# The gate tiles of the value pass: one split for each pair, ordered in the first of its two blocks

## The chip, the cores and the metric

The kernel runs on one core of a Trainium2 chip. The metric is the time of one execution in device microseconds (us), where lower is better. The engines are named as the profile names them: PE (TensorE, with PEld for its weight loads), DVE (VectorE), ACT (ScalarE), POOL (GpSimd) and SP (SyncE, which here only issues DMAs). Each engine works through its own instructions in the order in which the program issued them; an instruction whose inputs or buffer aren't ready holds up everything behind it on that engine.

## The reference, cut to what matters

Two trunk layers run over 256 prompt tokens and 32 sample tokens (8 sequences of 4). Each layer ends in a PEER mixer, which is where the change lies:

```python
q = (xb @ w_q).reshape(PEER_BLOCK, N_PEER_HEADS, 2, HALF_KEY)
s = jnp.einsum('thpd,hpnd->thpn', q, keys)
v1, i1 = lax.top_k(s[:, :, 0], TOPK_HALF)
v2, i2 = lax.top_k(s[:, :, 1], TOPK_HALF)
...                                         # 16 best of the 256 pairs: expert (128*i1 + i2), gate g
u = u_tab[expert]
v = v_tab[expert]
act = jax.nn.gelu(jnp.einsum('td,thkd->thk', xb, u), approximate=False)
return jnp.einsum('thk,thkd->td', g * act, v)
```

There are 16384 experts, 8 heads and 16 experts for each head and token. A table of experts has rows of 1024 numbers.

## The kernel before, in words

For 248 of the prompt tokens (`ND`, the "dense columns") the kernel does not gather experts. It computes the activation of every expert for every token as a dense product, multiplies by a gate that is zero where the expert wasn't chosen, and multiplies by the whole value table. The other 8 prompt tokens and the 32 sample tokens are done with gathered rows ("extra" and "sample").

**Blocks.** The tables come as 128 blocks of 128 experts, 512 KB each. Each block is split into two fp32r halves: ACT writes the high half `wh` (L234, cast) and DVE the low half `wl` (L235, subtract). The matmuls then run three times, high by high, high by low and low by high. There are three buffers for `wh` and `wl`; when block i is taken, block i+2 is split, so the ACT cast for i+2 waits until PE is done with block i-1.

**The U pass** (`kind == "u"`) multiplies block j of the first table by the 248 tokens: 24 matmuls of 128x248 into `pu` (L463 to L465). After each second block ACT applies the Gelu and writes the two columns of experts into `store` (L1340).

**The gates.** `gphase(c)` for the three chunks of blocks 0 to 45, 46 to 91 and 92 to 127 builds one-hot matrices of the chosen experts on DVE (`build`: L1249, L1251, L1253), multiplies them on PE into `pgt` (L1273, L1275) and multiplies `store` by the result on DVE (L1282). One round of matmuls for two groups of tokens and the DVE work on it is called a burst.

**The V pass** (`kind == "v"`) needs `store` as the moving operand, again in two halves: `wsplit(j)` writes `gh` (ACT, L439) and `gl` (DVE, L440) for blocks j and j+1 at once, 128x496, into one of two buffers each, and enters both halves of the pair in the list `gw`. `vmm` then does the 24 matmuls of a block (L1317 high, L1318 with `gl`, L1319 with `wl`) into four accumulators `acc`.

**The order of the blocks**, from `peer_order`: 82 U blocks (`RING`, the size of `store`), then two V and two U blocks in turn until U is at its end, then V alone. Blocks 126 and 127 of V are multiplied in the end stage (`vlast`).

**What sets the order of the rest.** After every block `pump` is called. It keeps two clocks of its own, `tp` for what PE has been given (2690 ns for a block) and `td` for what DVE has been given (1200 for a block, 620 for a `wsplit`, and a cost for each background step). While `td` is behind `tp` it issues the next background step: of the gate phases (`self.bg`), and, when those have to wait or are done, of the extra and sample work (`self.bg2`); in some blocks one step of the latter is issued in any case. So a DVE instruction stands in DVE's queue where `pump` or the block loop put it.

In the loop before, `wsplit(j - j % 2)` is called at the start of each V block. It does nothing when `j` is in `gw`. After a block `gw.pop(j)` takes the entry away, so at the start of an odd block the entry of the even one is missing and the pair is split a second time; then `wsplit(j + 1)` splits the next pair.

Of the kernel before, what the change touches and what calls it, by code (L numbers as in the profile page):

```python
# [201 lines left out]
class Stream:  # L202
# [39 lines left out]
    def next(self, src, idx, look=2):  # L242
        i = self.use_n
        self.use_n += 1
        assert self.items[i][0] is src and self.items[i][1] == idx, (i, self.items[i][1], idx)
        while self.split_n <= min(i + look, len(self.items) - 1):
            self._split()
        return self.hl.pop(i)


def peer_order():
    order = [("u", j) for j in range(RING)]
    u, v = RING, 0
    while v < 128:
        order += [("v", v), ("v", v + 1)]
        v += 2
        if u < 128:
            order += [("u", u), ("u", u + 1)]
            u += 2
    return order  # L260


class Kern:
# [867 lines left out]
    def peer(self, l):  # L1131
# [159 lines left out]
        gw = {}  # L1291

        def wsplit(j):
            c = [i for i, (j0, j1) in enumerate(CHUNKS) if j0 <= j < j1]
            if j in gw or not c or G[c[0]] in self.bg:
                return
            wh = wp.tile([128, 2, ND], F32R, name="gh", tag="gh", bufs=2)
            wl = wp.tile([128, 2, ND], F32R, name="gl", tag="gl", bufs=2)
            self.split_act(wh, wl, store[:, j % RING:j % RING + 2])
            self.td += 620  # L1300
            for i in range(2):
                gw[j + i] = (wh[:, i], wl[:, i])
# [8 lines left out]
        def vmm(j, w, d):  # L1311
            wh, wl = gw[j]
            vh, vl = w
            o = acc[d // 2][:, d % 2, :ND]
            f = j == 0 and d % 2 == 0
            e = j == 127 and d % 2 == 1
            nc.tensor.matmul(o, vh[:, d], wh, start=f, stop=False, skip_group_check=True)  # L1317
            nc.tensor.matmul(o, vh[:, d], wl, start=False, stop=False, skip_group_check=True)  # L1318
            nc.tensor.matmul(o, vl[:, d], wh, start=False, stop=e, skip_group_check=True)  # L1319

        for kind, j in peer_order():
            if kind == "v":
                if l == 0 and j in ADJ:
                    next(self.fg)
                for c, (j0, j1) in enumerate(CHUNKS):
                    if j == j0:
                        self.flush(G[c])
                wsplit(j - j % 2)
                if j % 2:
                    wsplit(j + 1)  # L1330
            if j >= 126 and kind == "v":
                continue
            w = self.wnext()
            if kind == "u":
                if j % 2 == 0:
                    pu = ps.tile([128, 2, NP], F32, name="pu", tag="mm", bufs=2)
                self.mm3(pu[:, j % 2, :ND], w, [(k, k) for k in range(KT)], aH, aL, 0, ND, True, True)
                if j % 2:
                    s = j % RING - 1
                    nc.scalar.activation(store[:, s:s + 2], pu[:, :, :ND], AF.Gelu)  # L1340
                done["u"] = self.udone = j + j % 2
                self.td += 1200
            else:
                if acc is None:
                    self.von = True
                    acc = [ps.tile([128, 2, NP], F32, name=f"acc{i}", tag="acc", bufs=4) for i in range(4)]
                for d in range(KT):
                    vmm(j, w, d)
                gw.pop(j)
                self.td += 1200  # L1350
            self.tp += 2690
            self.pump()
# [207 lines left out]
```

## Time and profile before

| | |
|---|---|
| median of 3 runs | 2377.87 us (2373.52 to 2379.7) |
| the profiled execution | 2358.28 us, of which the trace spans 2356.5 us |
| mean granted PE clock, profiled execution | 0.964 |
| first layer: U pass alone, then V pass | about 260 to 515 us, then 515 to 1164 us |
| second layer: U pass alone, then V pass | about 1432 to 1680 us, then 1680 to 2324 us |

The times are those of one core, and the profile is of one execution. In a row that groups instructions, the first number after the bar is their busy time in us, the second the mean of one in ns, and after the next bar stands how long their engine had been idle just before them and what ended that. In a row of a stretch of time, the numbers behind the length are the busy us of each engine (with the count), the granted PE clock as a share of full speed, the share of time in which the DMA engines were busy, and GB/s.

### The profile page before, as it was taken

How to read it: one execution, taken by the hardware profiler on the slowest of the kernel's cores; microseconds unless marked ns; L12 is line 12 of the kernel's file. 1: busy time of each engine (PE TensorE's matmuls, PEld its weight loads, DVE VectorE, ACT ScalarE, POOL GpSimd, SP SyncE). 2: the span in 40 equal slices, each digit the busy share in tenths (PEclk: the TensorE clock that was granted, in tenths of full speed). 3: DMA queues.
4: the chain of work that ended last, by engine and by line, in shares of the span. 5: the costliest groups of instructions: out<-in, count | busy, mean ns of one | idle time of the engine just before them, and what ended most of it. 6: DMA issues, size and time to landing. Idle time of an engine off the chain costs nothing. (4 is left out here: it accounts for less than half of the span.)

```text
span 2356.5 us, 46884 instructions
## 1 busy us (share of the span) xinstructions
PE 2085.2 (88%) x19266; PEld 1940.0 (82%) x19266; DVE 1752.2 (74%) x3496; ACT 981.7 (42%) x1341; POOL 256.9 (11%) x313
## 2 busy tenths in 40 slices
PE   7998999998888967788988889999988988778887
PEld 3787999998888857788976679999988888777887
DVE  3777997887777756678675679988876778666785
ACT  1845444344433323344441544444443434333443
POOL 1100004001000010012012100040020100000220
PEclk9999999999999989999999999999998999899998
DMA  9773458557665665569569645585575666544682
GB/s 356 267 285 131 148 193 287 171 171 232 208 203 192 204 197 153 161 196 325 152 185 280 225 131 155 186 302 171 170 255 177 213 200 211 158 129 125 226 287 82
DMA packets 131815, 477.11 MB, mean 202 GB/s; under 512 B 16032, under 2 KB 16544, under 8 KB 130960
## 3 DMA queue, kind: packets, MB, share of 16 engines
q1 hardware_dynamic: 93168, 334.09, 44.5%
q0 software_dynamic: 38432, 140.03, 17.8%
q8 instruction: 151, 2.47, 0.4%
q14 instruction: 64, 0.52, 0.1%
HBM read 466.63 MB, written 7.39 MB: 201 GB/s over the span
## 5 line engine op out<-in xcount | busy, mean ns | idle before, releaser
L235 DVE TENSOR_TENSOR wl<-raw,wh 128x1024 fp32r<-128x1024 f32 x583 | 708.3, 1220 | 324.3 <-ACT wh L234 323.4
L234 ACT CAST wh<-raw 128x1024 fp32r<-128x1024 f32 x583 | 609.7, 1047 | 637.9 <-PE acc L1318 411.3
L1318 PE MATMUL acc<-gl,wh 128*128 128x248 f32 x2048 | 603.7, 295 | 179.6 <-DVE gl L440 179.6
L1317 PE MATMUL acc<-gh,wh 128*128 128x248 f32 x2048 | 590.6, 288 | 7.7 <-ACT gh L439 7.7
L1319 PE MATMUL acc<-gh,wl 128*128 128x248 f32 x2048 | 589.0, 288 | 0.0
L465 PE MATMUL pu<-aH,wl 128*128 128x248 f32 x2048 | 569.7, 278 | 9.0 <-DVE wl L235 8.9
L1318 PEld LDWEIGHTS acc<-gl,wh 128*128 128x128 f32 x2048 | 406.6, 199 | 204.4 <-DVE gl L440 204.4
L463 PE MATMUL pu<-aH,wh 128*128 128x248 f32 x2048 | 573.3, 280 | 0.0
L464 PE MATMUL pu<-aL,wh 128*128 128x248 f32 x2048 | 571.1, 279 | 0.0
L1317 PEld LDWEIGHTS acc<-gh,wh 128*128 128x128 f32 x2048 | 406.7, 199 | 10.8 <-ACT gh L439 9.1
L1319 PEld LDWEIGHTS acc<-gh,wl 128*128 128x128 f32 x2048 | 407.5, 199 | 0.0
L465 PEld LDWEIGHTS pu<-aH,wl 128*128 128x128 f32 x2048 | 388.7, 190 | 10.8 <-DVE wl L235 10.7
L463 PEld LDWEIGHTS pu<-aH,wh 128*128 128x128 f32 x2048 | 387.3, 189 | 2.5 <-issue 2.1
L464 PEld LDWEIGHTS pu<-aL,wh 128*128 128x128 f32 x2048 | 388.0, 189 | 0.0
L439 ACT CAST gh<-store 128x496 fp32r<-128x496 f32 x254 | 153.2, 605 | 159.6 <-PE acc L1319 159.6
L440 DVE TENSOR_TENSOR gl<-store,gh 128x496 fp32r<-128x496 f32 x254 | 162.6, 668 | 21.1 <-ACT gh L439 20.7
L1340 ACT ACTIVATE store<-pu 128x496 f32<-128x496 f32 x128 | 74.9, 585 | 238.7 <-PE pu L465 238.7
L1282 DVE SCALAR_TENSOR_TENSOR store<-pgt,store 128x100 f32<-128x100 f32 (+3 forms) x192 | 86.8, 496 | 53.3 <-PE pgt L1275 52.4
L463 PE MATMUL prj<-aH,wh 128*128 128x288 f32 x392 | 119.9, 306 | 2.3 <-ACT wh L234 2.3
L1251 DVE TENSOR_TENSOR oA<-c,iT 128x1280 f16<-128x1280 f16 (+2 forms) x142 | 120.5, 849 | 0.0
L1369 POOL DMA_INDIRECT grow<-ur,ei x64 | 62.6, 978 | 514.4 <-DVE grow L1452 419.6
L464 PE MATMUL prj<-aL,wh 128*128 128x288 f32 x392 | 116.9, 298 | 0.0
(366 smaller groups left out, 2634.5 us busy)
## 6 DMA issues: line engine op xcount, KB each, us to landing
raw<-ut SPq DMA_DIRECT2D x256, 512.0 KB, 4.0
raw<-vt SPq DMA_DIRECT2D x256, 512.0 KB, 4.1
adaw<-wada POOLq DMA_DIRECT2D x56, 512.0 KB, 7.5
raw<-w SPq DMA_DIRECT2D x54, 512.0 KB, 5.9
raw<-wq SPq DMA_DIRECT2D x32, 512.0 KB, 4.3
adaw<-wada SPq DMA_DIRECT2D x18, 512.0 KB, 6.7
R<-us POOLq DMA_DIRECT2D x32, 286.5 KB, 9.2
store<-wada POOLq DMA_DIRECT2D x12, 512.0 KB, 5.2
```

The source lines that it names most:

```text
L234: nc.scalar.copy(hf, r)
L235: nc.vector.tensor_sub(lf, r, hf.bitcast(F32))
L439: self.nc.scalar.copy(h, src)
L440: self.nc.vector.tensor_sub(lo, src, h.bitcast(F32))
L463: nc.tensor.matmul(pt, h[:, kb], ah[:, ka, n0:n1], start=f, stop=False)
L464: nc.tensor.matmul(pt, h[:, kb], al[:, ka, n0:n1], start=False, stop=False)
L465: nc.tensor.matmul(pt, lo[:, kb], ah[:, ka, n0:n1], start=False, stop=e)
L1251: v.tensor_tensor(a, self.iota2[:, None].to_broadcast([128, g, 128, 2]), bc(0, 128), op=ALU.is_equal)
L1282: v.scalar_tensor_tensor(sv, pg[:, :n, q0 - j0:q1 - j0].rearrange("p t j -> p j t"), 1.0 / 4096.0, sv, op0=ALU.mult, op1=ALU.mult)
L1317: nc.tensor.matmul(o, vh[:, d], wh, start=f, stop=False, skip_group_check=True)
L1318: nc.tensor.matmul(o, vh[:, d], wl, start=False, stop=False, skip_group_check=True)
L1319: nc.tensor.matmul(o, vl[:, d], wh, start=False, stop=e, skip_group_check=True)
```

## The change

The list entry of an even block now stays until the odd block is done, when both are deleted. The call that splits the next pair is made within the even block, behind its matmuls and ahead of `pump`, and so ahead of the background step that `pump` may issue there.

```diff
                 for d in range(KT):
                     vmm(j, w, d)
-                gw.pop(j)
+                if j % 2:
+                    del gw[j - 1], gw[j]
+                else:
+                    wsplit(j + 2)
                 self.td += 1200
             self.tp += 2690
             self.pump()
```

The two calls of `wsplit` at the start of a block stay as they are; they now find the pair in the list, except at the first pair. With one split for a pair in place of two, `td` grows by 620 less for each pair, so `pump` issues background steps in earlier blocks: in the first layer the last gate burst of the third chunk moves from V block 86 to V block 75, and the last step of the sample work from V block 110 to V block 86.

On DVE, in the V blocks that have no U blocks between them, while the third chunk's gates are built. `gl` is the low half of the gates of a pair, `wl` that of a block of the table, L1282 the DVE end of a burst, and L1249 to L1253 a build. Before:

```order
L440 TENSOR_TENSOR gl<-store,gh 128x496 x2
L235 TENSOR_TENSOR wl<-raw,wh 128x1024 x2
L1282 SCALAR_TENSOR_TENSOR store<-pgt,store 128x36x12 x2
L1249 TENSOR_TENSOR oB_10818<-c_73,iT 128x432
L1251 TENSOR_TENSOR oA<-c_73,iT 128x1536
L1253 TENSOR_TENSOR oBs<-oB_10818,iG 128x864
L440 TENSOR_TENSOR gl<-store,gh 128x496 x2
L235 TENSOR_TENSOR wl<-raw,wh 128x1024 x2
```

The same place now:

```order
L235 TENSOR_TENSOR wl<-raw,wh 128x1024
L440 TENSOR_TENSOR gl<-store,gh 128x496
L235 TENSOR_TENSOR wl<-raw,wh 128x1024
L1282 SCALAR_TENSOR_TENSOR store<-pgt,store 128x36x12 x2
L1249 TENSOR_TENSOR oB_10946<-c_73,iT 128x432
L1251 TENSOR_TENSOR oA<-c_73,iT 128x1536
L1253 TENSOR_TENSOR oBs<-oB_10946,iG 128x864
L235 TENSOR_TENSOR wl<-raw,wh 128x1024
L440 TENSOR_TENSOR gl<-store,gh 128x496
```

Two `gl` stood together behind the burst's end and the build, the first of them for the block that PE was about to start; now one stands between the two `wl`, for the pair after the one that PE is in.

On ACT, in the first layer, where the sample's value rows begin (`sacc` is the copy of its partial sum out of PSUM, `gh` the high half of the gates, `wh` of a block). Before:

```order
L439 CAST gh<-store 128x496 x2
L234 CAST wh<-raw 128x1024 x2
L1471 COPY sacc<-so 128x512
L234 CAST wh<-raw 128x1024
L1340 ACTIVATE store<-pu 128x496
L234 CAST wh<-raw 128x1024
L439 CAST gh<-store 128x496 x2
```

Now:

```order
L439 CAST gh<-store 128x496
L1459 ACTIVATE sact<-sact 128x32
L234 CAST wh<-raw 128x1024
L1474 COPY sacc<-so 128x512
L234 CAST wh<-raw 128x1024 x2
L1340 ACTIVATE store<-pu 128x496
L234 CAST wh<-raw 128x1024
L439 CAST gh<-store 128x496
```

The second `gh` of each pair is gone, and the copy of the sample's sum has moved from U block 126 to V block 41, closer behind the activation of the sample's gates.

On DVE at that same turn (`sacd` is the sample's running sum on DVE, one row of experts after the other, each from a gathered `grow`). Before:

```order
L440 TENSOR_TENSOR gl<-store,gh 128x496 x2
L235 TENSOR_TENSOR wl<-raw,wh 128x1024 x2
L1480 TENSOR_SCALAR sacd<-grow,sact 128x1024
L1478 SCALAR_TENSOR_TENSOR sacd<-grow,sact,sacd 128x1024 x3
L235 TENSOR_TENSOR wl<-raw,wh 128x1024
L1282 SCALAR_TENSOR_TENSOR store<-pgt,store 128x36x12 x2
L1249 TENSOR_TENSOR oB_9993<-c_73,iT 128x432
```

Now:

```order
L235 TENSOR_TENSOR wl<-raw,wh 128x1024
L1483 TENSOR_SCALAR sacd<-grow,sact 128x1024
L1481 SCALAR_TENSOR_TENSOR sacd<-grow,sact,sacd 128x1024 x4
L235 TENSOR_TENSOR wl<-raw,wh 128x1024
L1481 SCALAR_TENSOR_TENSOR sacd<-grow,sact,sacd 128x1024
L235 TENSOR_TENSOR wl<-raw,wh 128x1024
L1481 SCALAR_TENSOR_TENSOR sacd<-grow,sact,sacd 128x1024
```

The sample's sums now follow one another block by block from here, where before a burst and two builds came between them.

## The prediction

> **What bounds the kernel now.** I read the page first, then the waits of PE's weight loads in each V pass, then DVE and ACT in order of time around one of these waits. The page's head says that PE carries the kernel, and that DVE is the next engine:
>
> ```profile
> span 2356.5 us, 46884 instructions
> PE 2085.2 (88%) x19266; PEld 1940.0 (82%) x19266; DVE 1752.2 (74%) x3496; ACT 981.7 (42%) x1341; POOL 256.9 (11%) x313
> ```
>
> The page's groups show where PE is idle. Nearly all of it stands before L1318, the matmul that needs `gl`, and DVE ends it. The same list gives the price of the two instructions that the change halves, and of the split of a table block:
>
> ```profile
> L235 DVE TENSOR_TENSOR wl<-raw,wh 128x1024 fp32r<-128x1024 f32 x583 | 708.3, 1220 | 324.3 <-ACT wh L234 323.4
> L234 ACT CAST wh<-raw 128x1024 fp32r<-128x1024 f32 x583 | 609.7, 1047 | 637.9 <-PE acc L1318 411.3
> L1318 PE MATMUL acc<-gl,wh 128*128 128x248 f32 x2048 | 603.7, 295 | 179.6 <-DVE gl L440 179.6
> L439 ACT CAST gh<-store 128x496 fp32r<-128x496 f32 x254 | 153.2, 605 | 159.6 <-PE acc L1319 159.6
> L440 DVE TENSOR_TENSOR gl<-store,gh 128x496 fp32r<-128x496 f32 x254 | 162.6, 668 | 21.1 <-ACT gh L439 20.7
> ```
>
> 254 splits are 127 in each layer: 64 pairs, of which 63 are split twice. A matmul's modelled end overlaps the next one, so a short wait hides in the busy time; the weight loads show it better. Their waits in the first V pass and then in the second (total, times, longest):
>
> ```profile
> PEld acc L1318 <- DVE gl L440: 101.3, 63, 9.1
> PEld acc L1317 <- ACT gh L439: 4.6, 3, 1.7
> PEld acc L1318 <- DVE gl L440: 103.1, 63, 7.8
> PEld acc L1317 <- ACT gh L439: 4.5, 3, 1.7
> ```
>
> 63 times in each layer is once for each second split: every odd block waits. Together 101.3 + 4.6 + 103.1 + 4.5 = 213.5 us. One of them in order of time, ACT, DVE and PEld:
>
> ```profile
> 960.41 0.61 ACT L439 CAST gh<-store 128x496 fp32r<-128x496 f32 x1 [1.32 <-PE acc L1319]
> 961.03 1.21 DVE L1282 SCALAR_TENSOR_TENSOR store<-pgt,store 128x432 f32<-128x432 f32 x2 [1.19 <-PE pgt L1275]
> 962.15 0.37 DVE L1249 TENSOR_TENSOR oB<-c,iT 128x432 f16<-128x432 f16 x1
> 962.44 0.95 DVE L1251 TENSOR_TENSOR oA<-c,iT 128x1536 f16<-128x1536 f16 x1
> 963.31 0.60 DVE L1253 TENSOR_TENSOR oB<-oB,iG 128x864 f16<-128x864 f16 x1
> 963.83 1.25 DVE L440 TENSOR_TENSOR gl<-store,gh 128x496 fp32r<-128x496 f32 x2
> 964.55 0.19 PEld L1318 LDWEIGHTS acc<-gl,wh 128*128 128x128 f32 x1 [2.95 <-DVE gl L440]
> ```
>
> The burst's end can't start before PE has done its matmuls, then comes a build, and only then the second split's `gl`, which the block that PE has already begun needs in its second matmul. PE stands 2.95 us.
>
> The waits have a second cost. Stretches of 10 us (and one of 115): the one with the wait above, one behind another wait, one without background work, and the U pass with gate bursts:
>
> ```profile
> 960.00:970.00 10.00, 7.24 (x86) 7.01 (x85) 5.19 (x8) 2.59 (x4) 0.00 (x0) 0.83 0.39 112
> 515.00:525.00 10.00, 8.75 (x60) 8.56 (x61) 6.45 (x8) 4.01 (x5) 0.00 (x0) 0.83 0.44 115
> 1135.00:1145.00 10.00, 10.00 (x84) 9.61 (x84) 6.16 (x8) 5.89 (x8) 0.00 (x0) 1.00 0.56 162
> 400.00:515.00 115.00, 113.62 (x1362) 112.93 (x1360) 100.64 (x141) 47.48 (x57) 2.38 (x2) 1.00 0.60 187
> 515.00:1170.00 655.00, 557.72 (x5270) 535.88 (x5271) 459.56 (x653) 259.58 (x330) 72.25 (x77) 0.96 0.64 203
> 1680.00:2338.00 658.00, 563.03 (x5328) 546.14 (x5326) 471.65 (x673) 260.67 (x332) 67.18 (x65) 0.96 0.60 191
> ```
>
> The granted clock falls to 0.83 around a wait, and is 1.00 where PE doesn't wait. Over both V passes it is 0.96.
>
> **The floor of a V pass.** In the U pass two blocks take 5.53 us (from one Gelu of a pair to the next; no burst lies between):
>
> ```profile
> 389.15 0.58 ACT L1340 ACTIVATE store<-pu 128x496 f32<-128x496 f32 x1 [1.82 <-PE pu L465]
> 394.68 0.59 ACT L1340 ACTIVATE store<-pu 128x496 f32<-128x496 f32 x1 [1.78 <-PE pu L465]
> ```
>
> A V block has the same 24 matmuls of 128x248, so 2.76 us. A V pass up to the end stage has 126 V and 46 U blocks: 172 x 2.76 = 475 us. Gate bursts, of which the U pass runs 13 of one chunk's in its last 115 us at PE 98% busy, add about 30 us for two chunks, the sample's matmuls about 10 and 5. That is 515 and 510 us; the passes last 649 (515 to 1164) and 644 us (1680 to 2324). So 134 + 134 = 268 us are above the floor; the 213.5 us of waits and 0.04 x 1313 = 53 us of clock account for 266. No more than that can be won.
>
> **The change, part by part.**
>
> *Second splits gone.* 126 `gh` x 0.605 = 76 us of ACT and 126 `gl` x 0.668 = 84 us of DVE. By themselves neither lies on the path, since both engines have idle time; what counts is that no block waits for a split made after it could have begun. The full 213.5 us goes, less what takes its place.
>
> *Next pair's split in the even block.* Its `gh` needs the buffer that the odd block of the pair before has left, and that block is done when the even block starts, so `gh` follows `wh` at once: 1.05 + 0.61 us after the block's start on ACT, `wl` and `gl` another 1.22 + 0.67 on DVE, some 3.6 us in all. It is needed two V blocks after that start, 5.5 us, and 11 us where U blocks lie between. Queued behind this `gh` is the next `wh`, which has to wait for the even block's end anyway; behind `gl` stands the burst, which waits for PE anyway. I cost it at nothing; the cover is those 1.9 us, and if it were gone each of 126 pairs would wait what it lacks.
>
> *Background steps earlier.* `td` grows by 620 less for a pair, and `pump` fills that with gate and sample steps. DVE's load in a block is then what `pump` aims at in the U pass too, where DVE is 100.64 us busy of 115. What is late next there is `wl`; the U pass of the first layer (its 255 us) shows how much:
>
> ```profile
> PEld pu L465 <- DVE wl L235: 5.6, 4, 3.7
> ```
>
> That is 2.2%; on 2 x 515 us it would be 23 us. Bounds: 0 (the stretch at 1135 us has no such wait) and 23. I take 15, nearer to the U pass, since the background work ends at block 86 to 95 and the rest of the pass runs without. The burst with its build before the next `wl` needs, from the rows above, 1.2 + 1.7 + 1.2 = 4.1 us from the burst's end, and that `wl` is needed two blocks later, at 5.5 us.
>
> *The sample's turn.* Here PE runs the sample's products, DVE its first sums, and both wait for gathered rows. It stays, with one more row on each (8 products and 5 sums in the first layer, 4 and 3 in the second):
>
> ```profile
> 856.87 0.75 DVE L1480 TENSOR_SCALAR sacd<-grow,sact 128x1024 f32<-128x1024 f32 x1 [15.80 <-DMA grow<-vt,ei]
> 870.87 0.57 PE L1318 MATMUL acc<-gl,wh 128*128 128x248 f32 x1 [8.87 <-DVE gl L440]
> PE acc L1318 <- DVE gl L440: 7.6, 1, 7.6
> 842.87 0.94 POOL L1369 DMA_INDIRECT grow<-vt,ei  x1 [9.92 <-PE so L1485]
> 862.07 0.94 POOL L1369 DMA_INDIRECT grow<-vt,ei  x1 [0.73 <-DVE sacd L1478]
> ```
>
> (The third row is that turn in the second layer; the last two are the first and the last of ten gathers in the first, 19.2 / 9 = 2.1 us from one to the next.) DVE stood 15.80 us for rows, and then PE 8.87 us for `gl`, because sums, a burst's end and two builds came first. Now PE will wait there for a `wl` behind the sums. Bounds for the two layers: 0, and the 8.9 + 7.6 = 16.5 us of before plus two more rows in each layer at 2.1 us, 25. I take 13, the middle, because no burst and no build comes between now.
>
> *Rows and table together.* In the stretches with a sum in nearly every block (about 55 blocks in all, with 52 gathered rows of 512 KB and 3 loads of the other table), 110 x 0.524 = 58 MB have to come in 55 x 2.76 = 152 us. The trace shows these rates at their highest and over the whole stretch of before:
>
> ```profile
> 1055.00:1065.00 10.00, 8.81 (x76) 8.60 (x75) 7.91 (x9) 4.67 (x6) 3.61 (x4) 1.00 0.99 374
> 1045.00:1118.00 73.00, 62.56 (x521) 60.40 (x520) 60.01 (x62) 34.07 (x44) 21.75 (x21) 1.00 0.91 322
> ```
>
> At 374 GB/s they need 155 us, at 322 180: 3 to 28 us more. I take 10, since 322 was at a DMA share of 0.91 with room left.
>
> *The clock.* 53 us are lost now; with waits at 38 of 213.5 us it could be all but 10, or, if other things hold it down, nothing. The U pass at 1.00 with 2% of waits is the nearer row. I take 25 of the 53, half, because a wait at each turn of a few blocks is enough to lose it.
>
> [...]
>
> *Sum.* 213.5 - 15 - 13 - 10 + 25 = 200 us. From the profiled execution, 2358 - 200 = 2158. The median of the runs, 2378, is 20 us above the profiled one, which I can't place and so leave as it is: 2378 - 200 = 2178 us.
>
> **The rivals.**
>
> 1. *The clock doesn't come back.* The sample's turn, which stays, has the lowest clock of both passes:
>
> ```profile
> 835.00:887.00 52.00, 34.15 (x288) 26.70 (x289) 23.82 (x31) 10.55 (x14) 9.37 (x10) 0.80 0.59 181
> 2008.00:2035.00 27.00, 18.86 (x211) 16.81 (x209) 13.65 (x20) 8.22 (x11) 5.42 (x5) 0.81 0.62 188
> ```
>
> That is 15 of the 53 us, for it; against it stands 1.00 over 115 us of U pass. The sum without its 25 is 175, so 2203 us. [...]
>
> 2. *DVE becomes the bound.* In the V pass DVE has 460 of 655 us now; less its half of the 84, and in 550 us, that is 76% on average, but `pump` will hold it at the U pass's 88% for the first 120 blocks. If each of the 126 pairs waited 0.8 us for a `wl` behind a burst, half of the mean wait of now (204.4 / 126 = 1.6), 100 us come back: 2278 us. Against it: the U pass at 88% DVE waits 5.6 us in 255.
>
> 3. *Slower: rows starve the table.* Gathers now start earlier, beside U and V blocks at full pace. The sum before this term is 210 us, so it decides where the 58 MB take 210 us more than the 152 that PE needs, below 58 / 362 = 160 GB/s; at 140 they take 414, and the kernel 2378 - 210 + 262 = 2430 us. The U pass alone draws 187 GB/s at a DMA share of 0.60, and 374 at 0.99 speaks against it.
>
> **How the numbers follow.** The forecast, 2178 us with 2140 to 2200 as its own range, gets 0.58. Rival 1, 2203 (2200 to 2235), 0.20; rival 2, 2278 (2235 to 2360), 0.17; rival 3 0.03; 0.02 for an end within 0.3% (7 us), about what a measurement of this kernel can tell from no change. The low end of the range is the floor's 268 us less the sample's turn and rows at their cheapest, 2378 - 268 + 20 = 2130; the high end, 2240, leaves out most of rival 2 and rival 3, two in ten. Faster by over 0.3%: 0.58 + 0.20 + 0.17 = 0.95.
>
> **What would show it.** In the profile after: `gh` and `gl` at 128 each; the waits of L1318 for `gl` at some single us, and those for `wl` not above 25 us in both V passes; the clock of the V passes at 0.98; the first at 550 to 570 us. A row of `wl` as the releaser of L1319 in nearly every odd block would show rival 2, waits of `wh` for `raw` rival 3. The forecast is wrong if a queue that I've not followed, PE's own order around the bursts above all, sets the pace once `gl` no longer does.

## The result, and the profile after

The changed kernel takes 2137.43 us (median of 4 runs, 2134.19 to 2141.6), the kernel before 2376.75 us beside it (4 runs, 2373.52 to 2379.7). The ratio is 0.8994, with a 95% interval of 0.8974 to 0.9015: 239 us less, where 200 were forecast. The profiled execution took 2138.45 us, with a span of 2136.7.

The head of the page, and some of its groups for the value pass:

```profile
span 2136.7 us, 46545 instructions
PE 2026.1 (95%) x19266; PEld 1898.0 (89%) x19266; DVE 1669.7 (78%) x3370; ACT 919.4 (43%) x1215; POOL 307.5 (14%) x313
...
L1318 PE MATMUL acc<-gl,wh 128*128 128x248 f32 x2048 | 573.1, 280 | 3.3 <-DVE gl L440 2.6
L1319 PE MATMUL acc<-gh,wl 128*128 128x248 f32 x2048 | 570.4, 278 | 5.0 <-DVE wl L235 5.0
L440 DVE TENSOR_TENSOR gl<-store,gh 128x496 fp32r<-128x496 f32 x128 | 85.4, 667 | 0.0
L439 ACT CAST gh<-store 128x496 fp32r<-128x496 f32 x128 | 77.2, 603 | 0.0
```

`gh` and `gl` are written 128 times, once for each pair. The idle time of PE ahead of L1318 is 3.3 us where it was 179.6, and PE is busy 95% of the span where it was 88%.

The waits of PE's weight loads in the first V pass (515 to 1056 us) and then in the second (1572 to 2109 us), without those that no other engine ended:

```profile
PEld so L1488 <- DMA grow<-vt,ei: 15.3, 7, 3.9
PEld acc L1319 <- DVE wl L235: 5.4, 2, 4.9
PEld pu L465 <- DVE wl L235: 2.0, 1, 2.0
PEld acc L1318 <- DVE gl L440: 1.8, 2, 1.4
PEld acc L1317 <- ACT gh L439: 1.4, 1, 1.4
...
PEld so L1488 <- DMA grow<-vt,ei: 6.2, 2, 5.0
PEld pu L465 <- DVE wl L235: 4.5, 2, 3.7
PEld acc L1318 <- DVE gl L440: 1.4, 1, 1.4
PEld acc L1317 <- ACT gh L439: 1.4, 1, 1.4
```

The 63 waits for `gl` in each pass have become 2 and 1. The largest part of what is left, 15.3 + 6.2 = 21.5 us, is the wait for the sample's gathered rows.

Stretches: both V passes, then the first one up to, in and behind the sample's turn, and 10 us with much DMA traffic. The five busy times are those of PE, PEld, DVE, ACT and POOL:

```profile
515.00:1056.00 541.00, 522.14 (x5215) 510.24 (x5216) 416.86 (x588) 226.78 (x267) 96.53 (x77) 0.98 0.74 244
1572.00:2109.00 537.00, 524.59 (x5304) 517.93 (x5303) 427.25 (x597) 231.01 (x271) 93.67 (x66) 0.99 0.71 235
515.00:765.00 250.00, 244.37 (x2510) 242.47 (x2511) 211.71 (x354) 108.32 (x131) 49.91 (x35) 0.99 0.73 241
765.00:775.00 10.00, 5.55 (x35) 2.76 (x35) 2.70 (x4) 0.60 (x1) 2.81 (x3) 0.97 0.94 340
775.00:785.00 10.00, 6.42 (x20) 0.70 (x16) 0.00 (x0) 0.00 (x0) 3.75 (x4) 0.67 0.61 200
785.00:795.00 10.00, 7.66 (x52) 6.95 (x50) 4.74 (x5) 4.61 (x6) 4.49 (x5) 0.84 0.72 227
795.00:805.00 10.00, 7.65 (x49) 7.66 (x50) 7.79 (x8) 1.26 (x2) 5.86 (x4) 0.67 0.85 264
805.00:1056.00 251.00, 250.49 (x2558) 249.71 (x2558) 189.92 (x220) 112.00 (x129) 29.71 (x27) 1.00 0.74 245
925.00:935.00 10.00, 10.00 (x90) 10.00 (x89) 9.48 (x9) 4.29 (x6) 6.21 (x5) 1.00 1.01 399
```

From the first V matmul to the end of block 125 the passes last 540 and 524 us (515.8 to 1056.0 and 1580.0 to 2104.0), where they lasted 649 and 639 (515.0 to 1163.8 and 1684.8 to 2323.5). That is 223 us less: all of the 220 us by which the span is shorter lie in them, and the stage between them takes 3 us more. (The windows of the second passes, 1572 to 2109 here and 1680 to 2324 before, are a few us wider.) Before and behind the sample's turn PE is busy nearly throughout at a clock of 0.99 and 1.00; the 40 us from 765 to 805 carry most of what is left.

### The profile page after: what moved, and what is told of

The parts are those of the page before. It is cut to its first block, busy times and chain, and to the rows that moved or that the text cites. A ratio compares the mean times of both kernels' runs of the same rounds, so it can differ in the third digit from the quotient of the medians.

```text
span 2136.7 us, 46545 instructions
## 1 busy us (share of the span) xinstructions
PE 2026.1 (95%) x19266; PEld 1898.0 (89%) x19266; DVE 1669.7 (78%) x3370; ACT 919.4 (43%) x1215; POOL 307.5 (14%) x313
## 4 chain that ended last, share of the span: by engine, by line
PE 61%; issue 17%; DVE 8%; DMA 6%; POOL 4%; ACT 3%; SPq 0%; POOLq 0%; DVEq 0%; ACTq 0%
PE acc L1317 8%; PE acc L1318 8%; PE acc L1319 8%; PE pu L465 7%; PE pu L463 7%; PE pu L464 7%; POOL grow L1372 4%; DMA grow<-vt,ei 3%; PE prj L463 2%; PE prj L464 2%; PE prj L465 2%; PE adap L402 2%; DVE wl L235 1%; PE prj L472 1%; PE pgt L1273 1%
## 5 line engine op out<-in xcount | busy, mean ns | idle before, releaser
L1317 PE MATMUL acc<-gh,wh 128*128 128x248 f32 x2048 | 574.8, 281 | 3.3 <-ACT gh L439 2.3
L1318 PE MATMUL acc<-gl,wh 128*128 128x248 f32 x2048 | 573.1, 280 | 3.3 <-DVE gl L440 2.6
L1319 PE MATMUL acc<-gh,wl 128*128 128x248 f32 x2048 | 570.4, 278 | 5.0 <-DVE wl L235 5.0
L1319 PEld LDWEIGHTS acc<-gh,wl 128*128 128x128 f32 x2048 | 390.1, 190 | 6.2 <-DVE wl L235 5.4
L1318 PEld LDWEIGHTS acc<-gl,wh 128*128 128x128 f32 x2048 | 389.1, 190 | 4.3 <-DVE gl L440 3.2
L1317 PEld LDWEIGHTS acc<-gh,wh 128*128 128x128 f32 x2048 | 389.4, 190 | 3.1 <-ACT gh L439 2.7
L1372 POOL DMA_INDIRECT grow<-ur,ei x64 | 92.3, 1442 | 362.5 <-DVE grow L1455 271.8
L1372 POOL DMA_INDIRECT grow<-vt,ei x64 | 89.3, 1396 | 249.6 <-DVE sacd L1481 178.2
L1282 DVE SCALAR_TENSOR_TENSOR store<-pgt,store 128x100 f32<-128x100 f32 (+3 forms) x192 | 86.9, 496 | 40.2 <-PE pgt L1275 39.5
L464 PE MATMUL prj<-aL,wh 128*128 128x288 f32 x392 | 116.2, 297 | 0.0
L465 PE MATMUL prj<-aH,wl 128*128 128x288 f32 x392 | 115.7, 295 | 0.0
```

The lines of the kernel that those rows point to most:

```text
L464: nc.tensor.matmul(pt, h[:, kb], al[:, ka, n0:n1], start=False, stop=False)
L465: nc.tensor.matmul(pt, lo[:, kb], ah[:, ka, n0:n1], start=False, stop=e)
L1282: v.scalar_tensor_tensor(sv, pg[:, :n, q0 - j0:q1 - j0].rearrange("p t j -> p j t"), 1.0 / 4096.0, sv, op0=ALU.mult, op1=ALU.mult)
L1372: self.nc.gpsimd.indirect_dma_start(out=r, out_offset=None, in_=tab, in_offset=bass.IndirectOffsetOnAxis(ap=ei[:, w, c:c + 1], axis=0))
```

## The experiments

Three theories of where the gain comes from. *Place*: the odd block waited because its split was issued at its start, behind the even block's background step; a split that stands earlier costs PE nothing, even if it is made twice. *Work*: the 160 us of casts and subtracts that are gone. *Bookkeeping*: `td` grows more slowly, so that the background steps come earlier.

**No step ahead of the second split.** The kernel before with all its 254 splits; after an even V block `pump` isn't called, after an odd one twice.

```diff
-            self.pump()
+            for _ in range(1 if kind == "u" else 2 * (j % 2)):
+                self.pump()
```

> The kernel before, with all its 254 splits and its prices, and the second split where it was, at the start of the odd block. Only the background steps are placed otherwise: none is issued after an even V block, and up to two calls' worth after an odd one, so no burst and no build stands on DVE ahead of the second split's gl. Theory of place (what the odd block waits for is the burst and the build ahead of its split, not the split): the waits of L1318 for gl fall from 204 us to what they are in before's tail without background work, about 0.2 us for each of 126 pairs, some 25 us, and some of the steps pushed together behind the odd block cost a few tens: 2180 to 2260 us. Theory of work (160 us of casts and subtracts on engines that are too full): nothing is taken away, 2360 to 2390. Theory of bookkeeping (the background work's earlier place in the pass made the gain): nothing is moved earlier by price, 2360 to 2390 too.

2246.09 us (2245.52 to 2249.16), ratio 0.9457 (0.9436 to 0.9477) to the 2377.0 us of before beside it: 131 us less, with no work taken away. The page's groups, the list of waits, and DVE and PEld in order of time at two odd blocks:

```profile
L440 DVE TENSOR_TENSOR gl<-store,gh 128x496 fp32r<-128x496 f32 x254 | 166.7, 672 | 40.9 <-ACT gh L439 39.9
...
PEld acc L1318 <- DVE gl L440: 116.2, 120, 6.6
...
1047.41 1.29 DVE L1479 SCALAR_TENSOR_TENSOR sacd<-grow,sact,sacd 128x1024 f32<-128x1024 f32 x1 [0.79 <-DMA grow<-vt,ei]
1048.61 1.22 DVE L235 TENSOR_TENSOR wl<-raw,wh 128x1024 fp32r<-128x1024 f32 x1
1049.75 1.25 DVE L440 TENSOR_TENSOR gl<-store,gh 128x496 fp32r<-128x496 f32 x2
1050.47 0.19 PEld L1318 LDWEIGHTS acc<-gl,wh 128*128 128x128 f32 x1 [1.13 <-DVE gl L440]
1056.25 0.19 PEld L1318 LDWEIGHTS acc<-gl,wh 128*128 128x128 f32 x1 [0.20 <-DVE gl L440]
```

The waits fell from 204.4 to 116.2 us, not to the 25 that I expected. The rows show why: the steps pushed together behind an odd block reach on DVE into the next even one (here two sums, of which the second waited 0.79 us for its row), so that `wl` and `gl` are late again and PE waits 1.13 us; where nothing had been left over, at 1056, it waits 0.20. So the time came out in the range of the place theory, but with only 88 us of waits gone. The clock can account for the rest: the runs of this kernel had a granted clock of 0.976 and those of before 0.957 (medians), by an estimate some 45 us. Moving the background steps away, and nothing else, gives these 131 us.

**Both splits, the second one early.** The changed kernel, but the entry is deleted after the even block too and the same pair split again there, ahead of `pump`: 254 splits, with their price in `td`. The next pair's split goes back to the start of the odd block.

```diff
                 else:
-                    wsplit(j + 2)
+                    del gw[j], gw[j + 1]
+                    wsplit(j)
```

> Two splits for each pair as before, 254 in all, with the same 620 for each in the planner's clock; only the second one is issued behind the even block's matmuls, ahead of the background step, instead of at the start of the odd block. The next pair's split stays at the start of the odd block. Place theory: nearly all of the waits for gl in odd blocks go, some in even blocks appear: 2150 to 2180 us. Work theory: nothing is saved, 2340 to 2377 us. Bookkeeping theory: the background steps stand where they stood before, 2340 to 2377 us.

2189.83 us (2188.92 to 2191.68), ratio 0.9236 (0.9193 to 0.9279); the kernel before took 2370.32 us beside it, so 180 us less, and 10 more than the place theory's upper end. A group of its page, and its waits:

```profile
L439 ACT CAST gh<-store 128x496 fp32r<-128x496 f32 x254 | 153.6, 605 | 174.1 <-PE acc L1319 174.1
...
PEld acc L1318 <- DVE gl L440: 61.5, 99, 1.4
```

The second split now ends at about the time at which the odd block needs it: PE waits 99 times, 86 of them in the 126 odd blocks, by 0.6 us in the mean and 1.4 at most, where it had waited 126 times by 1.6. It can't end much earlier: there are two buffers for `gh`, and 124 times ACT stands until an even block's last matmul (L1319) is done before it writes the second `gh`, 174.1 us in all. In the kernel before it was 122 times and 159.6 us; in the changed kernel `gh` waits for nothing (0.0 above). So of the 50 us or so that this kernel lacks to the changed one, at least a part is the buffer that a second split needs, which neither its place nor its price tells.

**Every split written twice, ahead of time.** The changed kernel with each split made twice into the same buffer, at the price of two.

```diff
-            self.split_act(wh, wl, store[:, j % RING:j % RING + 2])
-            self.td += 620
+            for _ in range(2):
+                self.split_act(wh, wl, store[:, j % RING:j % RING + 2])
+            self.td += 1240
```

> The changed kernel, but each split is written twice in place (254 gh and 254 gl, the second of each overwriting the first with the same data), with 1240 for it in the planner's clock: the work and the bookkeeping of before in the place of after. Place theory: 2137 to 2155 us, since the doubled gl is still ready a block ahead. Work theory and bookkeeping theory: near 2377 us, at least above 2300.

2166.74 us (2161.21 to 2171.97), ratio 0.9129 (0.9084 to 0.9174): 204 us less than before, with two more splits than before had, though 12 us above the place theory's range. From its groups and its waits (the matmul lines are one line further down than in the others):

```profile
L439 ACT CAST gh<-store 128x496 fp32r<-128x496 f32 x256 | 154.9, 605 | 325.6 <-DVE gl L440 325.6
...
PEld pf L1509 <- DVE sacd L1482: 21.1, 2, 12.6
PEld acc L1318 <- ACT gh L439: 15.6, 21, 3.6
PEld acc L1319 <- DVE gl L440: 14.8, 33, 0.5
```

The second cast has to wait until `gl` has read the first (325.6 us of ACT's idle time), and with that the split comes too late for some pairs: 15.6 + 14.8 us of waits. So a doubled split isn't free even ahead of time.

**The old bookkeeping.** One split for each pair, early, but `td` grows as before.

```diff
                 if j % 2:
                     del gw[j - 1], gw[j]
+                    self.td += 620
```

> The changed kernel, with 620 added to the planner's DVE clock in each odd block, so that the background steps stand in about the blocks in which they stood before. Place theory: 2137 us within 10, with the sample's sums later. Work theory: 2137 us within 10. Bookkeeping theory: the gain goes, 2340 us or more.

2125.06 us (2123.32 to 2131.48), ratio 0.897 (0.8926 to 0.9013): 245 us less. Its waits and the stretch of its first V pass:

```profile
PEld pf L1509 <- DVE sacd L1482: 12.8, 2, 7.8
...
515.00:1031.00 516.00, 514.48 (x5214) 505.25 (x5215) 412.29 (x584) 225.58 (x265) 100.90 (x76) 1.00 0.75 251
```

So the earlier background steps made none of the gain; in medians they cost 12 us, though the two ratios' intervals overlap. With the old prices PE doesn't wait for the sample's rows at all, and the first V pass lasts 516 us. What the changed kernel doesn't have is the end: `pf`, where the sample's sums are added up, waits 12.8 us for the last sum, and in the first layer PE comes to the end stage's V matmuls 18 us behind block 125, where the changed kernel needs 6. Against this kernel, the doubled splits have the same background prices and cost 0.9129 - 0.897 = 0.016 of 2370 us, 38 us. The work itself is worth no more than about that in this place, since the doubled split also waits for itself.

**One split, but late.** The changed kernel without the call in the even block; the next pair is split at the start of the odd block, behind the even block's background step.

```diff
-                else:
-                    wsplit(j + 2)
```

> One split for each pair as in the changed kernel, but the next pair's split stays where it was, at the start of the odd block, behind the background step of the even one. Place theory (the wait came from where the needed gl stood, behind a burst's end and a build): PE waits for gl only in even blocks that follow a burst with a build, up to about 1 us each, at most 15 us in a V pass: 2145 to 2165 us. Work theory (the 84 us of DVE and 76 us of ACT were what counted): the same work as the changed kernel, so 2137 us within 5. Bookkeeping theory (the gain came because the background steps moved to earlier blocks): 2137 us too.

2144.93 us (2139.75 to 2146.23), ratio 0.9037 (0.8994 to 0.9081). From its waits:

```profile
PEld pu L465 <- DVE wl L235: 23.4, 16, 4.6
...
PEld acc L1319 <- DVE wl L235: 7.0, 3, 6.0
PEld acc L1318 <- DVE gl L440: 5.8, 15, 1.4
```

The 15 waits for `gl` all stand in even blocks, as the place theory has it, but most are of 0.2 to 0.35 us. The time lies at the lower end of that theory's range. The call ahead of the burst is worth 0.004 of the time, within the intervals. Nearly all of the gain comes with the entry that stays: the one split that is left stood a block ahead of its use already.

**The sample's turn.** In order of time, PE, PEld and DVE of the changed kernel:

```profile
774.44 0.19 PEld L1488 LDWEIGHTS so<-grow,S 128*32 128x32 f32 x4 [3.87 <-DMA grow<-vt,ei]
780.88 0.14 PEld L1488 LDWEIGHTS so<-grow,S 128*32 128x32 f32 x4 [3.69 <-DMA grow<-vt,ei]
785.64 0.75 DVE L1483 TENSOR_SCALAR sacd<-grow,sact 128x1024 f32<-128x1024 f32 x1 [17.91 <-PE so L1488]
```

The eight products of the first layer are issued one behind the other, since each costs `td` nothing; PE's queue then stands behind rows that are still on their way, and DVE behind PE for 17.91 us. Two kernels spread this, and the changed kernel was run again beside them. The first prices a product:

```diff
-            yield 0
+            yield 1200
```

> The changed kernel with 1200 instead of 0 as the price of each of the sample's products on PE, so that one call of the planner issues one or two of them instead of eight or four at once. If the 21.5 us for which PE waits for gathered rows at the sample's turn, and the wl behind them, come from the products standing in one row in PE's queue: 15 to 25 us less than the changed kernel, 2112 to 2122 us. If the gathers themselves are too slow for any order there (512 KB each beside the table's 512 KB a block): no change, 2137 us.

The second leaves four of the eight products to DVE:

```diff
-CPS = (8, 4)
+CPS = (4, 4)
```

> The changed kernel with 4 instead of 8 of the sample's rows multiplied on PE in the first layer, as in the second, and 4 more summed on DVE. If the row of products costs in proportion to its length, the first layer's turn costs 8 to 12 us less: 2125 to 2129 us; if the sums on DVE behind it set the turn's end, no change.

> The changed kernel itself, as the measure for the others of this call: 2137 us.

The kernel before took 2378.61 us beside these, the changed one 2138.51 (2133.77 to 2145.27; ratio 0.8992, 0.8963 to 0.9021). Priced products give 2122.07 us (2116.65 to 2125.06), four products 2122.5 (2121.16 to 2125.31), each a ratio of 0.8916 (0.8889 to 0.8942): 16 us less, and none of their runs is as slow as the changed kernel's fastest. The first is at the upper end of what was expected, the second gained more than in proportion. The waits for rows, first of the changed kernel in the run beside these, then with priced products, then with four:

```profile
PEld so L1488 <- DMA grow<-vt,ei: 21.0, 10, 3.7
```

```profile
PEld so L1488 <- DMA grow<-vt,ei: 9.1, 4, 4.0
```

```profile
PEld so L1488 <- DMA grow<-vt,ei: 13.1, 5, 4.3
```

With priced products that is 11.9 us fewer of these waits, and a clock of 0.983 for 0.979 in the profiled runs.

**The old bookkeeping, and a sample step in each block.** Against the wait at the end, the kernel with the old prices was given one step of the sample's work in each of the blocks behind the gate phases, not in 27 of 32.

```diff
-BG3 = (27, 27)
+BG3 = (32, 32)
...
                 if j % 2:
                     del gw[j - 1], gw[j]
+                    self.td += 620
```

> The kernel of the old budget (e3) with the sample's steps issued in every block once the gate phases are done, instead of in 27 of 32. In e3 the end stage waits 12.8 us for the sample's last sums (two waits, one in each layer). If that wait is on the path, 8 to 14 us less than e3, about 2112 to 2117 us; if DVE can't carry a sum in every block beside wl and gl, the wait turns into waits of L1319 for wl and the time stays at 2125.

2115.75 us (2109.9 to 2117.07), ratio 0.8885 (0.8859 to 0.8912): 23 us below the changed kernel beside it, in the range expected, and the fastest of all. Stretches of its V passes:

```profile
515.00:1031.00 516.00, 511.78 (x5175) 501.24 (x5175) 413.08 (x584) 222.82 (x262) 104.76 (x77) 1.00 0.76 253
1568.00:2083.00 515.00, 513.48 (x5226) 507.38 (x5225) 418.93 (x590) 224.69 (x263) 94.37 (x65) 1.00 0.72 239
```

The wait of `pf` is no longer in its list, and the clock in both stretches is 1.00. From the first V matmul to the end of block 125 the passes last 521 and 515 us (514.6 to 1035.7 and 1560.1 to 2075.4).

## Why the prediction was right, and where its sizes were off

The 2137.43 us lie within the range of 2130 to 2240, but 3 us below the 2140 to 2200 that the forecast of 2178 had as its own. The mechanism held; several terms were off, in both directions.

**The waits.** Right: of 213.5 us for `gl` and `gh`, 1.8 + 1.4 + 1.4 + 1.4 = 6 us are left, so 207.5 went. The reason given was right as well: place alone gives 131 us with the split still late, 180 with it early, with all 254 splits made and paid for in `td`. It isn't the whole gain: the prediction looked at the buffer of `gh` for the next pair's split alone, but the second split had to wait for one too, up to the end of the even block, and that wait went with it.

**Second splits gone, "by themselves neither lies on the path".** Perhaps too strong. Doubled splits in the early place cost about 38 us, 0.16 of the gain, but part of that is the doubled split's wait for itself. The sum didn't suffer, since it counted the waits as a whole.

**Next pair's split, costed at nothing.** Right; `gl` makes PE wait three times in both passes. That it needs to stand ahead of `pump` at all was not shown (0.8994 against 0.9037).

**Background steps, 15 us of waits for `wl`.** The V passes have 5.4 + 2.0 + 4.5 = 11.9 us of such waits, but hardly any for the reason given. Only one of 0.7 us, at 1649, stands behind a burst's end and a build. One of 4.9 stands behind the sums of the sample's turn, at 797, and belongs to the next term. The other 6.3 us (at 575, 811 and 1864) follow steps that waited for gathered rows or a table block, and belong to the one behind it. Rival 2 falls with this, since it needed 100.

**The sample's turn, 13.** The place was right, the engine mostly wrong: I expected PE to wait there for a `wl` behind the sums, which it did for 4.9 us; but it waited 15.3 + 6.2 = 21.5 us for the rows themselves, where before had 10.7 and, on top, 8.9 + 7.6 for `gl` that are in the waits above. 10.8 us of these are new, so the term is 15.7. Before, too, `pump` issued the eight products one behind the other and PE waited for their rows; the sum gave PE's own wait for rows no price.

**Rows and table, 10.** Measured: the 6.3 us. The longest of these waits, on DVE and PEld, at a DMA share of 0.99 from 1850 to 1860 us:

```profile
1858.62 1.28 DVE L1481 SCALAR_TENSOR_TENSOR sacd<-grow,sact,sacd 128x1024 f32<-128x1024 f32 x1 [1.59 <-DMA grow<-vt,ei]
1861.17 1.28 DVE L1481 SCALAR_TENSOR_TENSOR sacd<-grow,sact,sacd 128x1024 f32<-128x1024 f32 x1 [1.27 <-DMA grow<-vt,ei]
1862.37 1.22 DVE L235 TENSOR_TENSOR wl<-raw,wh 128x1024 fp32r<-128x1024 f32 x1
1863.64 0.29 PEld L465 LDWEIGHTS pu<-aH,wl 128*128 128x128 f32 x1 [3.74 <-DVE wl L235]
```

The table itself was late four times, for ACT's casts, twice in each pass: 2.2 and 2.8 us, then 1.5 and 1.6. At 399 GB/s, at 925 us, PE was busy for the whole 10. Rival 3, which needed 210 us, falls with that.

**The clock, 25 of 53 us.** Too small. By the rows, 0.04 x (649 + 644) = 52 us were lost, and 0.02 x 541 + 0.01 x 537 = 16 are: 36 came back. (Some of the low clock falls into PE's waits, where it costs nothing; without that, the trace's clock records give 45 and 11, so 34.) Rival 1 is out. Half was a choice without a row; the U pass at 1.00, the nearer one, would have given nearly all.

That the length of a wait counts more than the number of waits is what the traces suggest: the kernel with the second split early has 99 waits of 1.4 us at most, and its V passes (516 to 1065 and 1601 to 2145 us) run at a clock of 1.00, where before's have 0.96 with 126. Of before's waits below 2 us, none of 54 in the second V pass and 8 of 55 in the first were followed by 6 us at a clock below 0.95; of those between 2.5 and 3.2 us it was 8 of 12 and 7 of 14. Together that is 15 of the 26 waits of 2.5 to 3.2 us; why the clock held behind the others, which were as long, was not shown.

**The sum.** 207.5 of waits, less 11.9 for `wl` and 10.8 for rows, and 36 of clock make 221 us; the profiled executions differ by 2358.28 - 2138.45 = 219.8. So the forecast of 200 was 20 too small by its own base. The background steps (14 too dear), the clock (11 too small) and rows and table (4 too dear) held it down, against 6 us of waits that stayed and 3 more at the turn.

**The 20 us that I couldn't place.** The other 19 of the 239 us. I had taken the profiled execution of before as typical but for a shift that stays; it wasn't typical. It had a granted clock of 0.964; the 23 runs of before timed beside the later kernels had 0.953 to 0.964, median 0.958, and their times go with it, from 2361.57 us at 0.963 to 2391.74 at 0.953. So the profiled one had a clock as high as the highest of them, and a typical run lost some 0.006 x 2378 = 14 us more clock. The changed kernel's profiled execution, at 0.977, lies among its runs. So 14 of the 19 us were probably more of the clock that the change gives back; the other 5, and why the clock varies from run to run of one kernel, stay open. That the size of the whole gain came within 39 us of the forecast owes something to the errors of the terms going both ways.

**What would show it.** `gh` and `gl` at 128, the waits for `gl` and `wl`, and a clock of 0.98 came as written; the first V pass, at 540 us, is a little below the 550 to 570. The floor of 515 and 510 us held: the last experiment's passes, with 521 and 515 us, come within some 6 us of it.

## What to carry to other kernels

On an engine that works in order, ask of each instruction not only what it costs but what stands ahead of it where it is issued: here the same split cost PE 204 us of waits behind the background step and 62 us ahead of it. When PE waits in many places for two or three microseconds, count the clock with the waits (36 us of it came back here, beside 207.5 us of waits), and look at its loss in several runs, since one profiled execution can lie at the edge of their spread (here at 0.964, where 23 runs had 0.953 to 0.964). And when a planner's prices decide the order, an instruction that waits for data should have a price, or the planner lines several of them up: a price for the products gave 16 us here.

## What the runs showed of the hardware

One core drew 399 GB/s over 10 us (DMA share 1.01) while PE was busy throughout at a clock of 1.00 and DVE for 9.48 of the 10 us; I had taken 374 as the highest rate. In the kernel with the second split early the V passes ran at a clock of 1.00 through 99 short waits, 61.5 us in sum and 1.4 at most; those of before, with 126 waits for `gl` of up to 9.1 us, ran at 0.96, which is 52 us.
